# A narrow value granule and a narrow third q, k granule joined into one wide granule beside the scan

## The chip, the core and the metric

The kernel runs on one core of one Trainium2 chip. The metric is the device time of one execution in microseconds (us), taken several times; smaller is better. The engines are called PE (TensorE: matmuls and transposes), PEld (its weight loads), DVE (VectorE), ACT (ScalarE), POOL (GpSimd) and SP (SyncE, which here only issues DMAs).

## The reference

One decoder layer on 512 tokens of width 1024. After an RMS norm there is one input projection `h @ w_in`, whose columns go to a state-space branch, to dilated attention and to gates:

```python
h = rms_norm(x, norm_w[layer])
proj = h @ w_in[layer].astype(f32)
u_s, z_s, q, k, v, z_a, r_s, r_a = jnp.split(proj, offsets, axis=-1)
y_s = s5_branch(u_s, ...)                          # scan over the tokens, GELU, GLU with w_glu
y_s = (y_s * jax.nn.silu(z_s)) @ w_ssm_out[layer]
q = apply_partial_rope(rms_norm(q.reshape(head_shape), q_norm_w ...), positions)
k = apply_partial_rope(rms_norm(k.reshape(head_shape), k_norm_w ...), positions)
y_a = dilated_attention(q, k, v)                   # 3 groups of 8 heads, head size 64
y_a = (y_a * jax.nn.silu(z_a)) @ w_attn_out[layer]
m = jax.nn.sigmoid(r_s) * y_s + jax.nn.sigmoid(r_a) * y_a
x = x + m @ w_o[layer]
```

Everything is float32. The attention has three groups of heads (0 is local, 1 and 2 are dilated), and the heads are worked on in four pairs.

## The kernel before

**Products.** Each float32 factor is split into a high and a low part, and a product is three matmuls, `mm3` (L133 to L136): high by high, high by low, low by high. Three kinds of work unit do the projection.

- `cm_unit` (L255) gives 128 output columns for all 512 tokens: 8 steps in the contraction by 3 matmuls, each 512 wide, with a piece of the weights standing in the array. It fills one PSUM bank. The units are called by name: `u`, `za`, `zs`, `v0`, `rs`, `ra`.
- `wide_granule` (L958) gives 512 output columns as tokens by columns: four steps of weights (`kq`) by four blocks of 128 tokens (`r`) by 2 by 3 matmuls, each 512 wide, 96 in all. Four PSUM banks stay open through it.
- `tok_granule` (L670) does the same for only 256 output columns: two steps (`kh`) by four blocks by 4 by 3 matmuls, each 256 wide, again 96 in all, in two banks.

**Weights.** `plan` (L138 to L188) lists all pieces of weights, 512 KB each, in the order of use. `get_w` (L195) takes the next one and asks for two more in advance: a DMA on SP into `w_raw` (two buffers, L210), the high part on ACT (L250), the low part on DVE (L252), both into three buffers.

**Order of work.** PE follows the order of the code strictly (`follow`, L62). The other engines' orders are planned at build time by the framework, which simulates a timeline and fills each queue as work becomes ready there. In the first half the list `order` (L161) strings projection units together, and `events` (L935 to L946) hangs pieces of the state-space branch between them at numbered places: a `cm_unit` has four places, a `tok_granule` eight. The scan itself is a chain on DVE (`step`, L732) beside the units `zs`, `v0` and `v`; from place Y0 = 88 on, `chunk` (L906) computes the outputs of the scan and turns and gates them. The last units there are `rs0` to `rs7` and `ra0`, `ra1`, the merge gates, which ACT puts through tanh and SP stores to DRAM (`gd` for rs, `rad` for ra).

**PSUM.** Eight banks are dealt round (`deal`, L85): three to projections (`p`) and five to the rest (`g`) in the first half; four and four from L1192 on.

**The middle.** At L1193 to L1242 the norm weights of q and k are fetched: broadcast for the rotary tables `tC`, `tS` (built on POOL, L1238 to L1242), and as six rows in `wq` (L1220 to L1223), which `turn_wcol` (L1224) turns into columns by one PE transpose of a 6 by 128 tile, in the second unit of the next loop. That loop (L1246 to L1256) is the GLU: 8 units with `w_glu`, whose results `yT` need `zl` (the stored z, read back, L1248) multiplied on POOL (L1250, L1251). Eight units with `w_ssm_out` follow (L1258 to L1262).

**Attention.** `qk_first` (L1028) is a wide granule for q and k of groups 0 and 1 of a head pair, with copies out of PSUM, sums of squares, and the norm and rotation on DVE (`qk_norm`, L978). For pairs 1 to 3 `qk_second` (L1040) is a second wide granule with q, k of group 2 and v of groups 1 and 2. For pair 0 this work is in two narrow pieces: `v_granule` (L698), beside the scan, and `qk_third` (L1053), right behind `qk_first`. Behind `qk_third` comes the unit `ra2`, with the transposes of q and k of group 0 (`qk_turn`, L1003) at its last place, and then the wide granule of pair 1, with the transposes of group 1, scores and softmax of pair 0 at its places (`scoring_first`, L1302).

Of the kernel before, what the change touches and what calls it, by code (L numbers as in the profile page):

```python
# [11 lines left out]
F32 = mybir.dt.float32  # L12
# [8 lines left out]
P = 128  # L21
D = 1024
S = 512
KT = D // P
NB = S // P
# [9 lines left out]
NG = 3  # L35
U0, ZS0, Q0, K0, V0, ZA0, RS0, RA0 = 0, 1024, 2048, 3584, 5120, 6656, 7168, 8192
# [16 lines left out]
def tile_hybrid_block(ctx: ExitStack, tc: tile.TileContext, x, positions, norm_w, w_in, lam_re, lam_im,  # L53
# [3 lines left out]
    act, dve, pool, sp = nc.scalar, nc.vector, nc.gpsimd, nc.sync  # L57
# [25 lines left out]
    dram = ctx.enter_context(tc.tile_pool(name="dram", bufs=1, space=DRAM))  # L83
    psum = ctx.enter_context(tc.tile_pool(name="psum", bufs=1, space=PSUM))
    deal = {"p": [0, 1, 2], "g": [3, 4, 5, 6, 7]}  # L85
# [22 lines left out]
    def bank(name):  # L108
        return ps_tile("g", name)

    def pj_tile():
        return ps_tile("p", "pj")

    def t2k(name, dtype=F32):
        return tmp.tile([P, 512], dtype, name=name, tag="t2k")
# [17 lines left out]
    def mm3(o, lh, ll, rh, rl, first, last):  # L133
        pe.matmul(o, lh, rh, start=first, stop=False, skip_group_check=True)
        pe.matmul(o, lh, rl, start=False, stop=False, skip_group_check=True)
        pe.matmul(o, ll, rh, start=False, stop=last, skip_group_check=True)  # L136

    plan, loaded, look = [], [], 2  # L138
    n_ra = 2
    WARM = 38  # L140

    def call(at, i):
        for n, f in at:
            if n == i:
                f()

    def section(w, k0, k1, *cols):
        return [w[0][k0 * P:k1 * P, c:c + n] for c, n in cols]

    def cm_spec(w, c0, kts=KT):  # L150
        return (section(w, 0, kts, (c0, P)), kts, P)

    def tok_spec(w, *cols):
        return [(section(w, 4 * h, 4 * h + 4, *cols), 4, 256) for h in range(2)]

    def wide_spec(w, *cols):
        return [(section(w, 2 * h, 2 * h + 2, *cols), 2, 512) for h in range(4)]

    for c in range(KT):
        plan.append(cm_spec(w_in, U0 + c * P))  # L160
    order = [("za", c) for c in range(NP)] + [("zs", c) for c in range(KT)] + [("v0", 0), ("v", 0)]  # L161
    order += [("rs", c) for c in range(KT)] + [("ra", c) for c in range(n_ra)]
    for kind, c in order:
        if kind == "v":
            plan += tok_spec(w_in, (V0 + 512, P), (V0 + 1024, P))
        else:
            plan.append(cm_spec(w_in, {"za": ZA0, "zs": ZS0, "rs": RS0, "ra": RA0, "v0": V0}[kind] + c * P))
    for c in range(KT):
        plan.append(cm_spec(w_glu, c * P))
    for c in range(KT):  # L170
        plan.append(cm_spec(w_ssm_out, c * P))
    def head(base, g, hp):
        return (base + g * 512 + hp * P, P)

    for hp in range(NP):
        plan += wide_spec(w_in, head(Q0, 0, hp), head(K0, 0, hp), head(Q0, 1, hp), head(K0, 1, hp))
        if hp == 0:
            plan += tok_spec(w_in, head(Q0, 2, hp), head(K0, 2, hp))
            plan.append(cm_spec(w_in, RA0 + n_ra * P))
        else:  # L180
            plan += wide_spec(w_in, head(Q0, 2, hp), head(K0, 2, hp), head(V0, 1, hp), head(V0, 2, hp))
            plan.append(cm_spec(w_in, V0 + hp * P))
# [12 lines left out]
    def get_w():  # L195
        i = taken[0]
        taken[0] += 1
        prefetch(i + 1 + look)
        return loaded[i]
# [66 lines left out]
    ident = cst.tile([P, P], F32, name="ident")  # L266
# [12 lines left out]
    hT_hi = cst.tile([P, KT, S], F32R, name="hT_hi")  # L279
    hT_lo = cst.tile([P, KT, S], F32R, name="hT_lo")  # L280
# [360 lines left out]
    def ra_unit(c, at=()):  # L641
        ps = cm_unit(hT_hi, hT_lo, at=at)
        th = gate_tile() if c <= n_ra else t2k("th")
        act.activation(th, ps, AF.Tanh, scale=0.5)
        sp.dma_start(rad[c], th)
# [21 lines left out]
    maskB_f = maskB.rearrange("p a k -> p (a k)")  # L667


    def tok_granule(at=()):  # L670

        pss = [pj_tile() for _ in range(2)]
        for kh in range(2):
            hi, lo = get_w()
            for b in range(2):
                for rr in range(2):
                    call(at, 4 * kh + 2 * b + rr)
                    r = 2 * b + rr
                    o = pss[b][:, rr * 256:(rr + 1) * 256]
                    for k in range(4):  # L680
                        kk = 4 * kh + k
                        mm3(o, hT_hi[:, kk, r * P:(r + 1) * P], hT_lo[:, kk, r * P:(r + 1) * P],
                            hi[:, k], lo[:, k], kh == 0 and k == 0 and rr == 0, kh == 1 and k == 3)
        return pss

    def v0_unit(hp, V, at=()):
# [8 lines left out]
            act.copy(V[:, 0].rearrange("p b c -> p (b c)"), pt)  # L695
        return finish

    def v_granule(hp, V, at=()):  # L698
        pss = tok_granule(at)
        for b in range(2):  # L700
            act.copy(V[:, 1:3, 2 * b:2 * b + 2], pss[b].rearrange("p (r g c) -> p g r c", r=2, g=2))

    def new_v():
        return big.tile([P, NG, NB, P], F32, name="V", tag="s6a")
# [69 lines left out]
    V = new_v()  # L774
    fin = []

    def filler(kind, c, at):
        if kind == "v0":
            fin.append(v0_unit(0, V, at))
        elif kind == "v":  # L780
            v_granule(0, V, at)
        else:
            {"u": u_unit, "za": za_unit, "zs": zs_unit, "rs": rs_unit, "ra": ra_unit}[kind](c, at=at)

    Mb = [dd[:, o:o + 1024].rearrange("p (g k) -> p g k", g=8) for o in (0, 1024, 2048)]
    idp = ident.rearrange("p (m two q) -> p two m q", two=2, q=Q)
# [159 lines left out]
    events = [e for _, e in events]  # L946
    b0 = 0
    for kind, c in [("u", j) for j in range(3, 8)] + order:
        n = 8 if kind == "v" else 4
        filler(kind, c, [(b - b0, f) for b, f in events if b0 <= b < b0 + n])  # L950
        b0 += n
    for b, f in events:
# [1 line left out]
    gT_hi, gT_lo = gTs  # L954
    if "gT" in dbg:
        sp.dma_start(dbg["gT"], gT_hi.bitcast(F32).rearrange("p k s -> p (k s)"))

    def wide_granule(th, tl, at=(), halved=False):  # L958

        pss = [pj_tile() for _ in range(NB)] + ([bank("pj")] if halved else [])  # L960
        for kq in range(4):
            hi, lo = get_w()
            for r in range(NB):
                call(at, 4 * kq + r)
                parts = [(pss[r], slice(0, 512))]
                if halved and r == NB - 1:
                    parts = [(pss[r], slice(0, 256)), (pss[NB], slice(256, 512))]
                for ps, c in parts:
                    for k in range(2):
                        kk = 2 * kq + k  # L970
                        mm3(ps[:, c], th[:, kk, r * P:(r + 1) * P], tl[:, kk, r * P:(r + 1) * P], hi[:, k, c], lo[:, k, c],
                            kk == 0, kk == KT - 1)
        return pss

    def new_raw(i):
        return big.tile([P, NB, 256], F32, name="qraw", tag=("s7a", "s7b")[i])
# [43 lines left out]
    def squares(sq, src):  # L1020
        n = src.shape[1]
        s = t2k("qsq")
        act.activation(s[:, 0:n], src, AF.Square)
        sv = s[:, 0:n]
        sv = sv.rearrange("p (h d) -> p h d", d=HD) if len(sq.shape) == 2 else sv.rearrange("p (r h d) -> p r h d", r=2, d=HD)
        dve.tensor_reduce(sq, sv, AX.X, ALU.add)
# [25 lines left out]

    def qk_third():  # L1053

        pss = tok_granule()
        raw = ptb[:, 0:2].rearrange("p a (b c) -> p (a b) c", c=256)
        sq = sml.tile([P, NB, 8], F32, name="ssq")[:, :, 0:4]
        for b in range(2):
            act.copy(raw[:, 2 * b:2 * b + 2].rearrange("p r c -> p (r c)"), pss[b])
            squares(sq[:, 2 * b:2 * b + 2], pss[b])  # L1060
        qk_norm((2,), [raw], sq)
        return raw

# [129 lines left out]
    rt, qt = t2k("rope"), t2k("qkw")  # L1193
# [23 lines left out]
    sp.dma_start(qkw[:, 1].rearrange("p g d -> p (g d)"),  # L1217
                 k_norm_w[0].rearrange("g d -> (g d)").unsqueeze(0).to_broadcast([P, NG * HD]))
    dve.tensor_scalar(qkw[:, 0], qkw[:, 0], -0.125, None, op0=ALU.mult)
    wq = qt[0:2 * NG, 384:512]  # L1220
    for a, w in enumerate((q_norm_w, k_norm_w)):
        for h in range(2):
            sp.dma_start(wq[a * NG:a * NG + NG, h * HD:h * HD + HD], w[0])  # L1223
    def turn_wcol():  # L1224
        wps = bank("wcp")
        pe.transpose(wps[:, 0:2 * NG], wq, ident[:2 * NG, :2 * NG])
        for a in range(2):
            dve.tensor_scalar(wcol[:, :, a], wps[:, a * NG:a * NG + NG], (-0.125, 1.0)[a], None, op0=ALU.mult)
        pool.memset(wcol[0:16], 1.0)
        pool.memset(wcol[64:80], 1.0)  # L1230
# [15 lines left out]
    for c in range(KT):  # L1246
# [5 lines left out]
        ps = cm_unit(gT_hi, gT_lo, at=[(2, turn_wcol)] if c == 1 else ())  # L1252
        th = t2k("gth")
# [4 lines left out]
    for c in range(KT):  # L1258
        r = t2k("rl")
        sp.dma_start(r, gd[1, c])  # L1260
        ps = cm_unit(yT_hi, yT_lo)
# [17 lines left out]
    ptb = big.tile([P, 4, 512], F32, name="ptb", tag="s6b")  # L1279
# [8 lines left out]
    Vs = {0: V}  # L1288
    raws = qk_first()
    raw = qk_third()  # L1290

    def turn(hp, g, a):
        return lambda: qk_turn(g, (raws[0], raws[1], raw)[g], *QK, turned=(a,))

    ra_unit(n_ra, [(3, turn(0, 0, 0)), (3, turn(0, 0, 1))])

    def scoring(hp, n, fin):
# [15 lines left out]
    for hp in range(NP):  # L1313
        if hp < NP - 1:
            raws = qk_first(scoring(hp, 3, fin) if hp else scoring_first(4))
            n = 3
            at = turning(hp, n) + [(n + 5, lambda hp=hp: values(hp))]
# [3 lines left out]
        else:  # L1321
# [3 lines left out]
            at = scoring(hp, 3, fin) + turning(hp, 16)  # L1325
# [9 lines left out]
    for cc in range(KT // 2):  # L1335
        hi, lo = get_w()
        pss = [pj_tile() for _ in range(2)]
# [6 lines left out]
        for c2 in range(2):  # L1344
            c = 2 * cc + c2
            if c in rals:
                th = rals[c]
            else:
                th = t2k("ral")
# [43 lines left out]
```

## Time and profile before

| what | value |
|---|---|
| runs, median (lowest to highest of 3) | 675.36 us (675.04 to 675.65) |
| the profiled execution's own time | 675.1 us |
| its span in the profile | 673.1 us |
| PE busy | 665.6 us, 99% of the span |
| DVE busy | 463.8 us, 69% |
| ACT busy | 322.6 us, 48% |
| POOL busy | 116.1 us, 17% |

The span is the time in which the program's instructions run; the execution's own time has 2.0 us more around it. In the timeline a row is: start, duration, engine, source line, operation, written tile, read tiles, shape, count, and in brackets the idle time ahead of it with what ended it. Matmuls overlap, so what one costs is read from the distance between two starts, not from its duration. Line numbers are those of the kernel before.

### The profile page before, as it was taken

What the parts mean: (1) busy time and instruction counts of PE and PEld (TensorE: products, weight loads), DVE (VectorE), ACT (ScalarE), POOL (GpSimd) and SP (SyncE); (2) the same over time, 40 slices, a digit from 0 to 9 for tenths busy, and PEclk for the clock granted to TensorE, in tenths of its full rate; (3) what the DMA queues carried; (4) which work ended last, traced back from release to release, by engine and by line L of the source; (5) the groups of instructions that cost most, each with busy time, mean ns of one, the idle gap of its engine ahead of it and who ended that gap; (6) DMA issues with size and microseconds to landing.
All of it is one profiled execution on the core that took longest, in us unless ns stands there. A gap on an engine that the chain in (4) does not pass through costs nothing.

```text
span 673.1 us, 12602 instructions
## 1 busy us (share of the span) xinstructions
PE 665.6 (99%) x4785; PEld 563.4 (84%) x4785; DVE 463.8 (69%) x965; ACT 322.6 (48%) x676; POOL 116.1 (17%) x273
## 2 busy tenths in 40 slices
PE   8999999999999999999999999999999999999997
PEld 8988888889887888888889888888888888888886
DVE  7999989999787365843248776658566856666631
ACT  6645544323566562421444664557356645633310
POOL 1010000600365238600000030012001200210000
PEclk9999999999999999999999999999999999999999
DMA  9666424643665543573243423223232213247231
GB/s 310 130 163 164 115 85 134 169 145 106 156 148 145 132 138 93 188 237 103 68 125 86 119 64 96 62 64 91 67 94 63 85 42 95 94 151 272 94 125 63
DMA packets 137380, 82.13 MB, mean 122 GB/s; under 512 B 32736, under 2 KB 125928, under 8 KB 137192
## 3 DMA queue, kind: packets, MB, share of 16 engines
q1 hardware_dynamic: 134968, 78.31, 39.6%
q0 software_dynamic: 2048, 2.36, 2.2%
q8 instruction: 38, 0.62, 0.4%
q10 hardware_dynamic: 304, 0.66, 0.3%
q14 instruction: 22, 0.18, 0.1%
HBM read 68.46 MB, written 10.49 MB: 117 GB/s over the span
## 4 chain that ended last, share of the span: by engine, by line
PE 88%; DVE 4%; issue 2%; POOL 2%; ACT 2%; DMA 1%; SPq 0%; ACTq 0%; POOLq 0%; DVEq 0%
PE pj L69 73%; PE sps L69 3%; PE yps L69 2%; PE ot L69 2%; PE ptp L74 2%; PE qtp L74 2%; DVE w_lo L252 1%; PE xps L69 1%; ACT w_hi L250 1%; PE wps L74 1%; DVE gth L1255 1%; DMA x_all<-in_x_dram 1%; PE kps L69 1%; DMA qkw<-in_q_norm_w_dram 1%; PE yT L74 0%
## 5 line engine op out<-in xcount | busy, mean ns | idle before, releaser
L250 ACT ACTIVATE w_hi<-w_raw 128x1024 fp32r<-128x1024 f32 x94 | 99.4, 1058 | 153.6 <-PE pj L69 130.9
L252 DVE TENSOR_TENSOR w_lo<-w_raw,w_hi 128x1024 fp32r<-128x1024 f32 x94 | 118.1, 1258 | 60.2 <-ACT w_hi L250 59.6
L69 PE MATMUL pj<-hT_hi,w_hi 128*128 128x512 f32 (+1 forms) x344 | 131.4, 384 | 0.0
L69 PE MATMUL pj<-hT_lo,w_hi 128*128 128x512 f32 (+1 forms) x344 | 128.8, 376 | 0.4 <-DVE hT_lo L355 0.4
L69 PE MATMUL pj<-hT_hi,w_lo 128*128 128x512 f32 (+1 forms) x344 | 126.7, 375 | 0.0
L69 PE MATMUL pj<-w_hi,hT_hi 128*128 128x512 f32 (+1 forms) x288 | 108.7, 377 | 0.0
L69 PE MATMUL pj<-w_hi,hT_lo 128*128 128x512 f32 (+1 forms) x288 | 105.6, 367 | 0.0
L69 PE MATMUL pj<-w_lo,hT_hi 128*128 128x512 f32 (+1 forms) x288 | 105.5, 366 | 0.0
L69 PEld LDWEIGHTS pj<-hT_hi,w_hi 128*128 128x128 f32 x344 | 64.7, 188 | 12.6 <-issue 1.3
L69 PEld LDWEIGHTS pj<-hT_lo,w_hi 128*128 128x128 f32 x344 | 64.8, 188 | 11.1 <-DVE hT_lo L355 0.6
L69 PEld LDWEIGHTS pj<-hT_hi,w_lo 128*128 128x128 f32 x344 | 63.7, 188 | 11.8
L69 PEld LDWEIGHTS pj<-w_hi,hT_lo 128*128 128x128 f32 x288 | 54.3, 189 | 9.1
L69 PEld LDWEIGHTS pj<-w_hi,hT_hi 128*128 128x128 f32 x288 | 54.4, 189 | 8.5 <-issue 0.5
L69 PEld LDWEIGHTS pj<-w_lo,hT_hi 128*128 128x128 f32 x288 | 54.5, 189 | 7.5
L1117 POOL COPY sw<-st 32x4 f32<-32x4 f32 x64 | 11.9, 186 | 175.0 <-ACT Pt L1073 172.2
L1018 DVE SCALAR_TENSOR_TENSOR qkp<-qtp,wcol,qkp 128x512 fp32r<-128x512 f32 (+1 forms) x32 | 23.6, 748 | 25.3 <-ACT qkp L1017 25.2
L1073 ACT ACTIVATE Pt<-Pt,st 128x256 f32<-128x256 f32 (+1 forms) x64 | 30.9, 484 | 19.8 <-DVE st L1071 19.8
L837 POOL DMA_DIRECT2D dd<-kt x64 | 33.8, 537 | 2.4 <-POOL kt L833 2.1
L1017 ACT ACTIVATE qkp<-qtp,wcol 128x512 fp32r<-128x512 f32 (+1 forms) x32 | 21.2, 683 | 23.0 <-PE qtp L74 20.8
L69 PE MATMUL pj<-w_lo,mT_hi 128*128 128x512 f32 (+1 forms) x72 | 26.3, 366 | 0.0
L69 PE MATMUL pj<-w_hi,mT_hi 128*128 128x512 f32 (+1 forms) x72 | 26.3, 366 | 0.0
L69 PE MATMUL pj<-w_hi,mT_lo 128*128 128x512 f32 (+1 forms) x72 | 26.3, 365 | 0.0
(299 smaller groups left out, 1180.6 us busy)
## 6 DMA issues: line engine op xcount, KB each, us to landing
w_raw<-in_w_in_dram SPq DMA_DIRECT2D x36, 512.0 KB
w_raw<-in_w_in_dram SPq DMA_DIRECT2D x112, 128.0 KB
w_raw<-in_w_glu_dram SPq DMA_DIRECT2D x8, 512.0 KB
w_raw<-in_w_ssm_out_dram SPq DMA_DIRECT2D x8, 512.0 KB
w_raw<-in_w_o_dram SPq DMA_DIRECT2D x8, 512.0 KB
w_early<-in_w_in_dram SPq DMA_DIRECT2D x4, 512.0 KB
ud<-uT SPq DMA_DIRECT2D x8, 256.0 KB
uss<-ud SPq DMA_DIRECT2D x8, 256.0 KB
```

The lines of the kernel that those rows point to most:

```text
L69: last[0] = nc.tensor.matmul(*a, **k)
L74: last[0] = nc.tensor.transpose(*a, **k)
L250: last_act[0] = act.activation(hi, raw, AF.Copy).ins
L252: dve.tensor_tensor(lo, raw, hi.bitcast(F32), op=ALU.subtract)
L837: pool.dma_start(M[Q * t:Q * t + Q, :, 0:P - Q * t], kt[:, :, t:].rearrange("q g k p -> q g (k p)"))
L1017: act.activation(hi, ps[sl], AF.Copy, scale=w)
L1018: dve.scalar_tensor_tensor(lo, ps[sl], w, hi.bitcast(F32), op0=ALU.mult, op1=ALU.subtract)
L1073: act.activation(o, o, AF.Exp, bias=nm, scale=-1.0, accum_out=st[:, kind, 1, h, b:b + 1])
L1117: pool.tensor_copy(sw[32 * r:32 * r + 32, :, :, b], st[32 * b:32 * b + 32, 1, :, :, r])
L1255: dve.scalar_tensor_tensor(th, th, 1.0, z, op0=ALU.add, op1=ALU.mult)
```

## The change

- In the first half the narrow value granule is replaced by a wide one, `qv_granule`, at the same place of the list. Its 512 columns are q and k of group 2 and v of groups 1 and 2 of pair 0. For its duration banks are dealt four and four. It has 16 places in place of eight. Its q, k half is copied to SBUF and stored to a DRAM tile `qd`, two DMAs of 256 KB; its v half is copied to `V` as before, in four copies in place of two.
- `qk_third` loses its granule: it reads `qd` back into the tile where its copies went before, and takes the sums of squares from there.
- The gate units `ra0` and `ra1` leave the end of the list; they now stand between `qk_first` of pair 0 and `ra2`. `rs6` and `rs7` come last in the list, and all events keep their place numbers.
- `wq` becomes a tile of 128 rows, set to zero by a memset on POOL ahead of its four small DMAs, and the transpose takes the whole 128 by 128 tile.
- `wide_granule` moves up in the file unchanged; `tok_granule` and `tok_spec` go.

```diff
-    order += [("rs", c) for c in range(KT)] + [("ra", c) for c in range(n_ra)]
+    order += [("rs", c) for c in range(KT)]
     for kind, c in order:
         if kind == "v":
-            plan += tok_spec(w_in, (V0 + 512, P), (V0 + 1024, P))
+            plan += wide_spec(w_in, head(Q0, 2, 0), head(K0, 2, 0), head(V0, 1, 0), head(V0, 2, 0))
...
         if hp == 0:
-            plan += tok_spec(w_in, head(Q0, 2, hp), head(K0, 2, hp))
-            plan.append(cm_spec(w_in, RA0 + n_ra * P))
+            plan += [cm_spec(w_in, RA0 + c * P) for c in range(n_ra + 1)]
...
-    def v_granule(hp, V, at=()):
-        pss = tok_granule(at)
+    qd = dram.tile([2, P, 512], F32, name="qd")
+
+    def qv_granule(V, at=()):
+        few = dict(deal)
+        deal.update(p=[0, 1, 2, 3], g=[4, 5, 6, 7])
+        pss = wide_granule(hT_hi, hT_lo, at)
+        deal.update(few)
         for b in range(2):
-            act.copy(V[:, 1:3, 2 * b:2 * b + 2], pss[b].rearrange("p (r g c) -> p g r c", r=2, g=2))
+            qs = t2k("qs")
+            for i in range(2):
+                r = 2 * b + i
+                act.copy(qs[:, 256 * i:256 * i + 256], pss[r][:, 0:256])
+                act.copy(V[:, 1:3, r], pss[r][:, 256:512].rearrange("p (g c) -> p g c", g=2))
+            sp.dma_start(qd[b], qs)
...
-        n = 8 if kind == "v" else 4
+        n = 16 if kind == "v" else 4
...
     def qk_third():
-        pss = tok_granule()
         raw = ptb[:, 0:2].rearrange("p a (b c) -> p (a b) c", c=256)
+        for b in range(2):
+            sp.dma_start(ptb[:, b], qd[b])
         sq = sml.tile([P, NB, 8], F32, name="ssq")[:, :, 0:4]
         for b in range(2):
-            act.copy(raw[:, 2 * b:2 * b + 2].rearrange("p r c -> p (r c)"), pss[b])
-            squares(sq[:, 2 * b:2 * b + 2], pss[b])
+            squares(sq[:, 2 * b:2 * b + 2], ptb[:, b])
...
-    wq = qt[0:2 * NG, 384:512]
+    wqt = qt[:, 384:512]
+    pool.memset(wqt, 0.0)
+    wq = wqt[0:2 * NG]
...
-        pe.transpose(wps[:, 0:2 * NG], wq, ident[:2 * NG, :2 * NG])
+        pe.transpose(wps[:, 0:P], wqt, ident)
...
+    for c in range(n_ra):
+        ra_unit(c)
     ra_unit(n_ra, [(3, turn(0, 0, 0)), (3, turn(0, 0, 1))])
```

More of the change, by code (lines that the diff above doesn't have):

```diff
@@ L151, in cm_spec @@
         return (section(w, 0, kts, (c0, P)), kts, P)
-    def tok_spec(w, *cols):
-        return [(section(w, 4 * h, 4 * h + 4, *cols), 4, 256) for h in range(2)]
     def wide_spec(w, *cols):
@@ L160, in tile_hybrid_block, with head @@
         plan.append(cm_spec(w_in, U0 + c * P))
+    def head(base, g, hp):
+        return (base + g * 512 + hp * P, P)
     order = [("za", c) for c in range(NP)] + [("zs", c) for c in range(KT)] + [("v0", 0), ("v", 0)]
-    order += [("rs", c) for c in range(KT)] + [("ra", c) for c in range(n_ra)]
+    order += [("rs", c) for c in range(KT)]
     for kind, c in order:
         if kind == "v":
-            plan += tok_spec(w_in, (V0 + 512, P), (V0 + 1024, P))
+            plan += wide_spec(w_in, head(Q0, 2, 0), head(K0, 2, 0), head(V0, 1, 0), head(V0, 2, 0))
         else:
@@ L171, in tile_hybrid_block @@
         plan.append(cm_spec(w_ssm_out, c * P))
-    def head(base, g, hp):
-        return (base + g * 512 + hp * P, P)
     for hp in range(NP):
@@ L667, in tile_hybrid_block, with wide_granule @@
     maskB_f = maskB.rearrange("p a k -> p (a k)")
-    def tok_granule(at=()):
-        pss = [pj_tile() for _ in range(2)]
-        for kh in range(2):
+    def wide_granule(th, tl, at=(), halved=False):
+        pss = [pj_tile() for _ in range(NB)] + ([bank("pj")] if halved else [])
+        for kq in range(4):
             hi, lo = get_w()
[L675 to L683, printed above, removed]
+            for r in range(NB):
+                call(at, 4 * kq + r)
+                parts = [(pss[r], slice(0, 512))]
+                if halved and r == NB - 1:
+                    parts = [(pss[r], slice(0, 256)), (pss[NB], slice(256, 512))]
+                for ps, c in parts:
+                    for k in range(2):
+                        kk = 2 * kq + k
+                        mm3(ps[:, c], th[:, kk, r * P:(r + 1) * P], tl[:, kk, r * P:(r + 1) * P], hi[:, k, c], lo[:, k, c],
+                            kk == 0, kk == KT - 1)
         return pss
@@ L780, in filler @@
         elif kind == "v":
-            v_granule(0, V, at)
+            qv_granule(V, at)
         else:
-            {"u": u_unit, "za": za_unit, "zs": zs_unit, "rs": rs_unit, "ra": ra_unit}[kind](c, at=at)
+            {"u": u_unit, "za": za_unit, "zs": zs_unit, "rs": rs_unit}[kind](c, at=at)
     Mb = [dd[:, o:o + 1024].rearrange("p (g k) -> p g k", g=8) for o in (0, 1024, 2048)]
@@ L956, in tile_hybrid_block @@
         sp.dma_start(dbg["gT"], gT_hi.bitcast(F32).rearrange("p k s -> p (k s)"))
[L958 to L973, printed above, removed]
     def new_raw(i):
```

## The prediction

> **What bounds the kernel now.** First the page's head and its busy table.
>
> ```profile
> span 673.1 us, 12602 instructions
> PE 665.6 (99%) x4785; PEld 563.4 (84%) x4785; DVE 463.8 (69%) x965; ACT 322.6 (48%) x676; POOL 116.1 (17%) x273
> ```
>
> PE is idle for 7.5 us in all, so only PE's own work, or a wait on PE that grows, can move the end. Next the busy time by windows, for the narrow value granule, the wide `qk_first` of pair 0 and the narrow third granule. The window edges are starts of PE rows, so a window's length is what that granule costs PE.
>
> ```profile
> core 0: us, PE busy (x) PEld busy (x) DVE busy (x) ACT busy (x) POOL busy (x), PEclk, DMA share, GB/s
> 147.65:159.59 11.94, 11.94 (x101) 11.94 (x100) 11.35 (x13) 3.75 (x5) 0.00 (x0) 1.00 0.44 134
> 330.68:352.44 21.76, 21.76 (x97) 18.02 (x96) 6.87 (x7) 12.44 (x21) 0.00 (x0) 1.00 0.32 94
> 352.44:363.95 11.51, 11.51 (x97) 11.51 (x96) 10.15 (x24) 4.24 (x7) 0.00 (x0) 1.00 0.25 70
> ```
>
> All three are PE without a gap, at a full granted clock (1.00). 96 matmuls 512 wide take 21.76 us, 0.2267 each; 96 that are 256 wide take 11.51 us, 0.1199 each, a little over half. The first window holds four transposes more (`vtp`, the finish of `v0`), whence 11.94. Last the chain of work that ended last, in order of time.
>
> ```profile
> 151.12 19.54 PE pj L69 x120
> ...
> 236.90 1.07 ACT w_hi L250
> 237.99 1.24 DVE w_lo L252
> 239.67 0.57 SPq L1205
> 240.29 4.21 DMA qkw<-in_q_norm_w_dram
> ...
> 291.27 0.70 DVE yT_lo L123
> 292.01 76.21 PE pj L69 x380
> ```
>
> Through both places where narrow granules stand (147 to 160 and 352 to 364) the chain is PE itself. Between 236.90 and 292.01 it is not: it leaves PE at the end of the last unit but one, and runs through a weight load and the position and norm-weight loads on SP (by the code, the rotary tables on POOL and the GLU's POOL work hang on these) to the low part of `yT`, and back to PE at 292.01.
>
> **The change part by part. The granules.** Removed are 192 narrow matmuls, 2 x 11.51 = 23.02 us of PE; added are 96 wide ones, 21.76 us. That is 1.26 us less PE work: half of the matmuls, each of which carries a fixed part. (The two widths give it: 0.2267 - 2 x 0.1199 = -0.013, so 13 ns a matmul, and 96 fewer are 1.26 us.) `ra0` and `ra1` cost the same wherever they stand. By place: up to the end of the list PE loses the narrow 11.51 and two units of 24 x 0.2267 = 5.44, and gains 21.76, so it gets there 0.63 us earlier; behind `qk_first` it loses 11.51 and gains 10.88, again 0.63.
>
> The Trainium skill prices this otherwise: "TensorE: Matmul & The Clock Gate", section "Back-to-back issue gap", gives a warm gap of N / 2.4 + 2.5 ns, which as an estimate makes 0.109 and 0.216 us of the two widths and 0.24 us of this part. The trace's 0.1199 and 0.2267 do not agree, and they decide; what is left of it is rival 4.
>
> **The whole turn of the norm weights.** The timeline of PE at that transpose, and at the four full transposes in the value granule:
>
> ```profile
> 250.79 0.39 PE L69 MATMUL pj<-gT_hi,w_lo 128*128 128x512 f32 x1
> 251.11 0.22 PE L74 MATMUL wcp<-ident,qkw 6*128 6x6 f32 x1
> 251.26 0.50 PE L69 MATMUL pj<-gT_hi,w_hi 128*128 128x512 f32 x1
> 251.60 0.39 PE L69 MATMUL pj<-gT_lo,w_hi 128*128 128x512 f32 x1
> ```
>
> ```profile
> 150.52 0.60 PE L74 MATMUL vtp<-ident,vt 128*128 128x128 f32 x4
> 150.88 0.36 PE L69 MATMUL pj<-w_hi,hT_hi 128*128 128x256 f32 x1
> 151.07 0.28 PE L69 MATMUL pj<-w_lo,hT_hi 128*128 128x256 f32 x1
> ```
>
> From 250.79 to 251.60 there are 0.81 us where two matmul steps take 0.45: the six-row transpose costs 0.36. From 150.52 to 151.07 there are 0.55 us, of which one narrow step is 0.12: four full transposes cost 0.43, 0.11 each. So PE saves 0.25 us. But this lies in the stretch where the chain is not PE, and the weight loads of PE show its end:
>
> ```profile
> 292.01 0.19 PEld L69 LDWEIGHTS pj<-yT_lo,w_hi 128*128 128x128 f32 x1 [0.52 <-DVE yT_lo L123]
> ```
>
> PE waits there for the last low part of `yT`, and nothing in that chain reads the turned weights on the way. If PE arrives 0.25 earlier, the wait becomes 0.77. I take nothing for this edit; its bounds are 0 and -0.25. The memset on POOL stands ahead of the four small loads on SP, behind which wait the first `zl` load and the next weights:
>
> ```profile
> 239.96 1.29 POOL L1250 TENSOR_TENSOR gsum<-gT_hi,gT_lo 128x512 f32<-128x512 f32 x1 [15.12 <-issue]
> ```
>
> POOL is idle for 15 us ahead of this, so the memset runs as soon as its buffer is free; even behind this row it would hold SP up by no more than its 1.29 us, which the 4.21 us of the `qkw` load above, the one the tables wait for, hides.
>
> **The wide granule beside the scan.** Three things could stall PE. First, four banks in place of two. The deal's count puts the first tile into the bank of `zs7`, whose last reader is a DVE row, in a stretch where DVE is 95% busy (11.35 of 11.94). Second, the scan must be done by `chunk(0)`, and third, the coefficients for the kernels `kps` behind it.
>
> ```profile
> 145.13 0.68 DVE L621 SCALAR_TENSOR_TENSOR z<-th,pj 128x512 f32<-128x512 f32 x1
> ...
> 164.50 0.69 DVE L742 TENSOR_TENSOR Xs<-Xs,scn 128x512 f32<-128x512 f32 x1
> ...
> 169.83 0.76 DVE L424 TENSOR_TENSOR ab<-ab 128x576 f32<-128x576 f32 x1
> ```
>
> ```profile
> 171.91 1.16 PE L69 MATMUL yps<-ab,Xs 64*64 64x64 f32 x64
> 173.00 0.66 PE L69 MATMUL kps<-ab,dd 64*16 64x128 f32 x32
> ```
>
> The bank is free at 145.81 and needed at 147.65: 1.84 us to spare, and nothing ahead of it changes. The scan ends at 165.19 and is needed at 171.91, the coefficients end at 170.59 and are needed at 173.00: 6.7 and 2.4 us to spare, less the 0.63 that PE comes earlier. DVE has as many low parts to make per us as before. All three cost nothing; the last, with 1.8 us left, would be next to show.
>
> The copies out of PSUM become eight of half the width:
>
> ```profile
> L1049 ACT COPY V<-pj 128x256 f32<-128x256 f32 x12 | 4.6, 383 | 0.0
> ```
>
> 8 x 0.383 = 3.06 us of ACT, which was busy for 3.75 of 11.94. The first bank is dealt again to `rs0`, but its last matmul lies 3 x 1.36 = 4.08 us ahead of that, time for its two copies. The two stores of `qd` stand on SP like the gate stores, ahead of weight pieces that are needed two units (10.9 us) later. Nothing on the path: 0.
>
> **Behind `qk_first`.** Its norm must be done at the transposes of group 0:
>
> ```profile
> 363.30 0.41 DVE L1001 TENSOR_TENSOR qraw<-rt,rt 128x256 f32<-128x256 f32 x1
> ```
>
> ```profile
> 368.07 1.03 PE L74 MATMUL qtp<-ident,qraw 128*128 128x128 f32 x8
> ```
>
> It has 4.4 us to spare; PE comes 0.63 us earlier, 3.7 are left, while the third's squares, sums and norm may now start sooner and stand between. Two sums of squares already do. The loads of `qd` wait for stores of 190 us ago. Cost 0; what is left of DVE's load moves off the start of pair 1, where PE does not wait for it.
>
> **Sum.** -1.26 us from the granules and 0 from all else. The profiled execution took 675.1 us, 673.1 in the span and 2.0 around it, 0.3 below the median of 675.36 and within its runs. From the median: 675.36 - 1.26 = 674.1 us, -0.19%. A measurement of this kernel can tell some 0.2%, 1.35 us, from no change; the forecast lies just short of that line, 674.01.
>
> **The rivals.**
> 1. *The turn counts too.* If the stretch up to 292 is a little shorter in the new order, PE's 0.25 us and part of the 0.52 wait come on top: 675.36 - 1.26 - 0.25 = 673.85, and at best 673.3, with all of the 0.52. For it: the wait is small. Against: the chain is tied to the same PE event as before.
> 2. *Slower: the z loads wait for the gate stores.* `rs7` now stores into `gd` at the end of the list, just before the first `zl` load reads the same DRAM tile; before, `ra1` stored to another tile there. If the load were held until that store has landed, the chain would lengthen:
>
> ```profile
> 243.45 0.35 SPq L1248 DMA_DIRECT2D zl<-gd  x1
> 245.31 0.35 SPq L645 DMA_DIRECT2D rad<-th  x1
> ```
>
> ```profile
> 246.33 2.23 POOL L1251 TENSOR_TENSOR zl<-zl,gsum 128x512 f32<-128x512 f32 x1 [5.09 <-DMA zl<-gd]
> 249.61 0.25 POOL L1240 TENSOR_TENSOR tS<-rope,qkw 128x32 f32<-128x32 f32 x1 [1.05 <-ACT rope L509]
> ```
>
> A load takes 2.9 us from issue to use; I take the same for a store. All 0.63 earlier: store at 244.7, landed at 247.6, load used at 250.5, multiply done at 252.7. The tables stand behind it on POOL (second row), at 249.0 in the new order; they would start 3.7 us late, and PE's wait at 292 would grow by that: 674.1 + 3.7 = 677.8. The kernel is slower than before once they start over 1.3 us late. Against it, on the same queue at the read-back of `rad`:
>
> ```profile
> 369.42 0.47 SPq L1324 DMA_DIRECT2D th<-rad  x1
> 371.86 0.34 SPq L645 DMA_DIRECT2D rad<-th  x1
> ```
>
> There a load of one slice goes ahead of the store of another, so slices do not wait for each other.
> 3. *One stage gives its share back.* If DVE is late by 2.4 us or so beside the scan, or by over 3.7 behind `qk_first`, one of the 0.63 goes: 674.1 + 0.63 = 674.7.
> 4. *The wide matmuls are no cheaper there.* If beside the scan, with DVE 95% busy where the wide window has 32%, a wide matmul took as long as two narrow ones, 96 x 0.2398 = 23.02 us, the granules would give nothing: 675.4. Against it: the two narrow windows have DVE at 95% and 88%, and both run at 0.1199 (11.94 less the 0.43 of the transposes is 11.51). By the page named above it would be 675.36 - 0.24 = 675.1.
> 5. *No gain.* The queues are planned anew by the build's simulation; a wait of 1 to 2 us anywhere eats the gain: 675 to 676.
>
> **How the numbers follow.** Forecast 0.45, at 674.1, with a range of its own from 673.7 to 674.5 for the spread of the runs (0.3 us to either side of the median), and 0.21 of the 0.45 beyond the line of 674.01. Rival 1 0.25 (0.24 beyond the line), rival 2 0.07, rival 3 0.12, rival 4 0.04, rival 5 0.07, of which 0.04 is slower by over 0.2%. Faster by over 0.2%: 0.21 + 0.24 = 0.45. Slower: 0.07 + 0.04 = 0.11. Within: the rest, 0.44. The range of 673.2 to 675.7 reaches from the best of rival 1 to the middle of rival 5, and leaves out rival 2 and half of rival 5.
>
> **What would show it.** Right: no 256-wide rows at the value granule, whose window is 21.8 + 0.4 = 22.2 us without a PE gap; three `ra` units behind `qk_first`; `chunk(0)` some 0.6 us earlier, `qtp` of pair 0 some 1.3 earlier; the wait for `yT_lo` near 0.8; a whole transpose at 0.11. Wrong: a PE wait inside the wide granule or before `kps`, a wait at the first `qtp`, tables on POOL starting later than 249.0, or an end that moves by less than the two windows do.

## The result and the profile after

The changed kernel takes 672.58 us (median of 20 runs, 671.73 to 677.93) against 675.24 (20 runs, 674.30 to 678.72) for the kernel before beside it: 2.66 us less by the medians, which is a ratio of 0.9961. The ratio on record, which goes by more than the medians, is 0.9968 with an interval of 0.9953 to 0.9982, so a gain of 2.2 us, between 1.2 and 3.2. The forecast of 674.1 was too small a gain, and the result lies below its range. (The forecast's ratio, 0.9981, is just inside this interval; experiment 1, with 0.9943 to 0.9974, and the profiles show that the rest is real.) The profiled execution took 671.95 us, its span is 670.1 after 673.1. The page's head, and the window of the new granule with its four transposes:

```profile
span 670.1 us, 12439 instructions
PE 663.3 (99%) x4689; PEld 557.8 (83%) x4689; DVE 463.3 (69%) x965; ACT 322.7 (48%) x680; POOL 116.1 (17%) x274
```

```profile
core 0: us, PE busy (x) PEld busy (x) DVE busy (x) ACT busy (x) POOL busy (x), PEclk, DMA share, GB/s
147.71:169.96 22.25, 22.25 (x101) 18.22 (x99) 20.89 (x25) 7.22 (x12) 0.00 (x0) 1.00 0.36 106
```

PE has no gap in the wide granule, and 22.25 us is the 22.2 of the prediction, with DVE busy for 20.89 of them. PE's busy time is down by 2.3 us and its idle time by 0.7 (7.5 to 6.8), though its wait for `x` at the start is 0.5 longer in this execution.

To see where 3.0 us of span went, the chain is compared by stages: the starts of the same pieces, before and after, and what the changed kernel is ahead by.

| piece of the chain | before | after | ahead |
|---|---|---|---|
| outputs `yps` of `chunk(0)` | 171.04 | 170.50 | 0.54 |
| `yps` of `chunk(4)` | 206.12 | 205.58 | 0.54 |
| `yps` of `chunk(5)` | 214.82 | 212.92 | 1.90 |
| the chain leaves PE (`w_hi` on ACT) | 236.90 | 235.01 | 1.89 |
| back on PE behind `yT_lo` | 292.01 | 289.83 | 2.18 |
| first `qtp` of pair 0 | 368.23 | 365.42 | 2.81 |
| last long stretch of PE | 603.59 | 600.80 | 2.79 |

The two lots of the granules are there: 0.54 in the first half (0.60 from the starts of the two granules, 147.65 and 147.71; 0.63 was worked out) and 0.63 between 292 and 368. The surprise is 1.36 us between two chunks, in code that the change does not touch. There, the chain of before, and then that of the changed kernel (start, length, what, number of instructions):

```profile
206.12 2.02 PE yps L69 x96
208.14 0.34 PE kps L69 x10
208.49 0.96 issue
209.45 0.62 PE kps L69 x22
210.07 4.32 PE pj L69 x18
```

```profile
205.58 2.02 PE yps L69 x96
207.60 0.59 PE kps L69 x32
208.19 4.30 PE pj L69 x18
```

In the kernel before, PE stops after 10 of the 32 small matmuls `kps` and waits for nothing that the profile knows ("issue"). From the start of `kps` to the next `pj` it takes 1.93 us (208.14 to 210.07), in the changed kernel 0.59: the stop costs 1.34 us. The profile of before had shown it: the full chain has the row of 0.96 us, and the list of PE's waits has this line as the second of its four (us in total, times, longest), which is missing in the list of the changed kernel:

```profile
PE kps L69 <- issue: 1.0, 1, 1.0
```

So 1.26 + 1.34 = 2.60 us, near the 2.66 of the medians and inside the interval of 1.2 to 3.2, which is too wide to tell more. The GLU stretch gave 0.29 more in the two profiled executions; experiment 1 shows that this part changes from one execution to another.

The theory to test: the stop is a late fetch of PE's own instructions. In the DMA records a queue marked "instruction" brings PE's program in packets of 16 KB, one for each 256 instructions, and a matmul is two instructions (load and multiply). In the trace the stop at `kps` always lies at PE's instruction 4033, counted from 0 in order of start; the stops of experiments 10 and 12 below lie at 4289, one block of 256 later. The DMA by queue of the kernel before, from PE's entry into the block ahead (instruction 3777, at 203.55) on, in two windows, 203.55 to 206.95 and 206.95 to 209.45:

```profile
q0 software_dynamic: 95, 0.17, 43.4%
q1 hardware_dynamic: 266, 0.33, 29.0%
```

```profile
q1 hardware_dynamic: 1140, 0.51, 71.4%
q0 software_dynamic: 139, 0.11, 13.7%
q8 instruction: 1, 0.02, 2.2%
```

In the first 3.4 us no instruction packet is moved; the packet starts at 207.00, lasts 0.88 us, and 1.57 us after its end PE goes on, at 209.45. In the chunks, whose 128 tiny matmuls are 256 instructions, a block is used up in about 5 us (203.55 to 208.49); between them 24 large matmuls, 48 instructions, take 5.44. The change moves where the blocks end: the wide granule has 16 places where the narrow one had eight, so the chunks stand two units, 96 instructions, earlier in PE's program. The rivals: the matmuls `kps` themselves, the queues as planned anew, the gate units' new place, or data on the DMA engines.

### The profile page after: what moved, and what is told of

It is laid out like the page before. It is cut to its first block, busy times and chain, and to the rows that moved or that the text cites. A ratio compares the mean times of both kernels' runs of the same rounds, so it can differ in the third digit from the quotient of the medians.

```text
span 670.1 us, 12439 instructions
## 1 busy us (share of the span) xinstructions
PE 663.3 (99%) x4689; PEld 557.8 (83%) x4689; DVE 463.3 (69%) x965; ACT 322.7 (48%) x680; POOL 116.1 (17%) x274
## 4 chain that ended last, share of the span: by engine, by line
PE 88%; DVE 4%; issue 2%; DMA 2%; ACT 2%; POOL 1%; SPq 0%; ACTq 0%; DVEq 0%; POOLq 0%
PE pj L69 73%; PE sps L69 3%; PE yps L69 2%; PE ot L69 2%; PE ptp L74 2%; PE qtp L74 2%; DVE w_lo L248 1%; PE xps L69 1%; ACT w_hi L246 1%; PE wps L74 1%; DVE gth L1247 1%; DMA x_all<-in_x_dram 1%; PE kps L69 1%; DMA qkw<-in_q_norm_w_dram 1%; PE yT L74 0%
## 5 line engine op out<-in xcount | busy, mean ns | idle before, releaser
L69 PE MATMUL pj<-w_hi,hT_hi 128*128 128x512 f32 x256 | 103.1, 403 | 0.0
L69 PE MATMUL pj<-w_hi,hT_lo 128*128 128x512 f32 x256 | 100.0, 390 | 0.0
L69 PE MATMUL pj<-w_lo,hT_hi 128*128 128x512 f32 x256 | 99.9, 390 | 0.0
L69 PEld LDWEIGHTS pj<-w_hi,hT_lo 128*128 128x128 f32 x256 | 48.0, 188 | 10.3
L69 PEld LDWEIGHTS pj<-w_hi,hT_hi 128*128 128x128 f32 x256 | 48.1, 188 | 9.6 <-issue 0.5
L69 PEld LDWEIGHTS pj<-w_lo,hT_hi 128*128 128x128 f32 x256 | 48.2, 188 | 8.7
```

The costliest lines, as they stand in the source:

```text
L69: last[0] = nc.tensor.matmul(*a, **k)
```

## The experiments

**1 and 2. One part at a time.** The changed kernel with the six-row transpose put back, and the kernel before with the whole one.

```diff
...
-        pe.transpose(wps[:, 0:P], wqt, ident)
+        pe.transpose(wps[:, 0:2 * NG], wq, ident[:2 * NG, :2 * NG])
```

> The kernel after, with the six-row turn of the norm weights put back (no memset, a 6 by 128 transpose). It separates the two edits. If the turn's 0.25 us of PE time is swallowed by the wait for the last low part of yT, as the prediction took it, the time is that of the kernel after, 672.6, within 0.1; the wait falls from 0.5 to some 0.25. If the turn counts, the time is 672.8 to 672.9. In both cases the 0.96 us gap of PE in the middle of the kps matmuls at 208.5 stays away, because the number of PE instructions ahead of it is that of the kernel after.

> The kernel before, with only the whole turn of the norm weights. The gap of 0.96 us at kps (209.45) stays, since nothing ahead of it changes. If the yT chain swallows the turn: 675.2, the same as before, with a yT_lo wait of 0.77 in place of 0.52. If the turn counts: 675.0. Nothing here can explain more than 0.25 us.

Without the whole turn: 672.82 us (7 runs), ratio to before 0.9958 (0.9943 to 0.9974). With it alone: 674.81 (12 runs), 0.9999 (0.9985 to 1.0013). The turn is worth nothing that can be measured, and the whole gain is the granule's and the gate units'. In the first of them PE has gaps of 0.36 and 0.22 us at the end of the GLU (290.66 and 291.39), with another releaser (`yT_hi`, 0.8 us) than the changed kernel's `yT_lo`: this end moves by tenths from one execution to another. The stop at `kps` is gone in the first and there in the second (0.69 us, again at instruction 4033).

**3 and 4. Other instruction counts ahead of the chunks.** More of the transposes that warm PE up at the start: 48 more in the changed kernel, which puts back the 96 instructions that it has lost ahead of the chunks; 80 more (118 in place of 38) in the kernel before.

```diff
-    WARM = 38
+    WARM = 86
```

> The kernel after, with 48 more warm-up transposes at the start (86 in place of 38): as many PE instructions more as the list has fewer ahead of chunk 0 in the new order (two units of 24). Theory, late instruction fetch: the gap inside kps depends on where the blocks of PE's instructions begin against the dense small matmuls of the chunks; with the old count restored the gap of about 1 us comes back in the same chunk. Then the time is 672.6 + 48 x 0.11 - 1.3 (PE's idle time ahead of hps) + 1.4 = 678.0. Rival, the gap came of what the other queues and DMAs did at that moment in the old order: these are as in the kernel after, so no gap, and 676.6.

> The kernel before, with 80 more warm-up transposes (118 in place of 38): 160 PE instructions, which in blocks of 256 puts the chunks where they stand in the kernel after (96 fewer). Late instruction fetch: the gap inside kps goes, and the time is 675.2 + 80 x 0.11 - 0.8 - 1.4 = 681.8. Rival, the old order of transfers makes the gap: it stays at kps of the same chunk, and the time is 683.2.

The changed kernel takes 678.73 us (8 runs; 1.0056, 1.0036 to 1.0076), and the stop is back, at instruction 4033 as before:

```profile
213.21 0.41 PE L69 MATMUL kps<-ab,dd 64*16 64x128 f32 x10
214.86 0.62 PE L69 MATMUL kps<-ab,dd 64*16 64x128 f32 x22 [1.24 <-issue]
```

The kernel before takes 682.23 us (4 runs; 1.0102, 1.0081 to 1.0124), and its stop is gone, with nothing of the chunks changed:

```profile
215.99 0.66 PE L69 MATMUL kps<-ab,dd 64*16 64x128 f32 x32
216.57 0.50 PE L69 MATMUL pj<-hT_hi,w_hi 128*128 128x512 f32 x1
```

So it is the position in PE's program, in both directions. `kps` as such, the wide granule and the new queues are out as causes: experiment 4 has the narrow granules and the old queues, experiment 3 the new ones. The times lie nearer to this theory's 678.0 and 681.8 than to 676.6 and 683.2.

**5 and 6. The data of the weight load.** The load of 512 KB that SP issues at 204.45 us, just after PE has entered block 3777, is doubled by a copy into a tile that nobody reads, and then cut to an eighth. The second of these leaves out seven eighths of the weights of the gate unit `ra1`.

```diff
...
+        if i == 32:
+            spare = dram.tile([KT * P, P], F32, name="spare")
+            with tc.issue_after(d.ins):
+                sp.dma_start(spare, srcs[0])
```

```diff
+        if i == 32:
+            sp.dma_start(raw[:, 0:1], srcs[0][0:P].rearrange("(k p) c -> p k c", p=P))
+            raw = raw[:, 0:1].broadcast_to([P, kts, cols])
...
```

> The kernel before, with a second copy of the weight piece that is loaded at 204.45 us (512 KB, from DRAM to DRAM, into a spare tile that nothing reads) issued on SP just behind that load; PE's instructions and all other queues are as before. Theory (PE's 0.96 us gap at its instruction 4033 is a late fetch of instructions, held up by the data on the DMA engines): before, the packet of the fetch starts 3.45 us after PE has entered the block ahead; with twice the data from 204.5 us on it starts 1 to 2 us later, the gap grows to 2 to 3 us, and the kernel takes 676.2 to 677.2 us. If fetch packets go ahead of data that is already queued, the gap stays and so does the time. Rival (the gap is something of the matmuls kps themselves, or of the position in the program alone): gap 1.0, 675.2.

> The kernel before, where that same load at 204.45 us brings an eighth of the piece (64 KB in place of 512) and the split reads that eighth eight times; it leaves out seven eighths of the weights of one gate unit. PE's instructions and the order of all queues are as before. Theory (late fetch behind data): the packet of the fetch starts 1 to 2.5 us after PE has entered the block ahead, as most do, the gap of 0.96 us is gone or under 0.2, and the kernel takes 674.2 to 674.4. Rival (kps itself or the position alone): gap 1.0, 675.2.

Neither moved the fetch as the theory had it. With twice the data 676.40 us (10 runs; 1.0015, 1.0000 to 1.0029), which is inside the 676.2 to 677.2 expected, but not by a longer stop; with an eighth 675.43 (10 runs; 1.0001, 0.9988 to 1.0014). The packet starts 3.40 and 3.67 us after PE's entry (3.45 before), and the stop is 0.69 and 0.96 us. So the fetch is not late because of this load, and that half of the theory fell. It does not clear data on the DMA engines in general: from PE's entry to the start of the packet, the hardware queue q1 moved 0.34 MB before, 0.30 in experiment 5 and 0.32 in experiment 6, so the two edits hardly changed the data ahead of the packet.

**7 and 8. The gate units' place, and the place of the chunks.** The changed kernel with `ra0`, `ra1` back at the end of the list; and that kernel with the chunks eight places later, so that as many PE instructions stand ahead of each as before.

```diff
-    order += [("rs", c) for c in range(KT)]
+    order += [("rs", c) for c in range(KT)] + [("ra", c) for c in range(n_ra)]
...
-    for c in range(n_ra):
-        ra_unit(c)
...
```

```diff
-    W0, K0B, V0B, Y0 = 16, 49, 74, 88
+    W0, K0B, V0B, Y0 = 16, 49, 74, 96
```

> The changed kernel with its two gate units put back to the end of the list beside the scan, so of the change the wide granule and the whole turn remain. The wide granule takes 16 places of the list where the narrow one took 8, so the chunks still stand two units earlier than before and PE's instructions up to the last chunk are those of the changed kernel. Theory (late fetch, set by where the blocks of instructions end): no gap at kps, 672.6 us like the changed kernel, and 672.1 to 672.6 if the wait for the low part of yT goes, since PE has two units more ahead of it. Rival (the gate units' place is what took the 1.4 us away): the gap is back and the kernel takes 673.6 to 674.0.

> The kernel of the run above (wide granule, gate units in the list), with the chunks eight places of the list later, so that they stand between the same units as before and as many PE instructions stand ahead of each as before. Theory (late fetch): the gap is back at instruction 4033, 0.7 to 1.4 us, and the kernel takes 673.3 to 674.0 us, which is the kernel before less the 1.26 us of the granules. Rival (the wide granule or the new queues took the gap away): no gap, 672.6.

On the stop both expectations hold: none in the first, and in the second

```profile
218.50 0.41 PE L69 MATMUL kps<-ab,dd 64*16 64x128 f32 x9
219.88 0.62 PE L69 MATMUL kps<-ab,dd 64*16 64x128 f32 x23 [0.97 <-issue]
```

On the times both miss by far: 680.52 us (4 runs; 1.0074, 1.0051 to 1.0096) and 682.20 (4 runs; 1.0101, 1.0073 to 1.0128), both slower than the kernel before. Most of the cause stands in one row of PE's timeline (experiment 7):

```profile
371.64 1.94 PE L74 MATMUL qtp<-ident,qraw 128*128 128x128 f32 x8 [6.46 <-DVE qa L129]
```

With nothing but three quarters of one unit between `qk_first` and the transposes of group 0, PE waits 6.46 us for the norm and rotation on DVE. Behind this wait the granted clock is 0.50 instead of 1.00 until 375.89 (third figure from the end):

```profile
371.64:375.89 4.25, 4.25 (x14) 3.61 (x15) 3.89 (x15) 1.52 (x3) 0.00 (x0) 0.50 0.00 0
```

From these transposes to the next ones (375.92) PE takes 4.28 us, in the changed kernel 2.26 (365.26 to 367.52): another 2.0 us. Wait and clock make some 8.5 us in this execution; by the medians experiment 7 takes 7.9 us more than the changed kernel. In experiment 8 the wait is as long, and the granted clock stays at 0.50 until 379.02. Before, the narrow third granule (11.5 us) stood there; the change fills the place with the two gate units (10.9 us). That is what "gate units in their place" is worth: without it, the wide granule makes the kernel 5.4 us slower than before.

**9 and 10. POOL's transfers later.** Something else stands at the same place in the six kernels with the stop above (before, experiments 2, 3, 5, 6 and 8): POOL issues eight transfers of the kernel block `kt` into `dd`, and PE enters block 3777 0.3 to 0.6 us after their start.

```profile
202.96 4.21 POOL L837 DMA_DIRECT2D dd<-kt  x8 [0.30 <-POOL kt L833]
```

Here POOL first multiplies that block (j = 5) by 1.0, twice, in the kernel before and in the changed one.

```diff
+        if j == 5:
+            for _ in range(2):
+                pool.tensor_scalar(kt, kt, 1.0, None, op0=ALU.mult)
         M = Mb[j % 3]
```

> The kernel before, in which POOL multiplies the fifth kernel block kt by 1.0 twice before it issues that block's eight transfers into dd, so that this issuing (202.96 to 207.17 us before, 4.21 us) starts some 2 to 4 us later; PE's instructions are as before. Theory (the late fetch stands behind POOL's issuing: in all six kernels with the gap POOL starts those eight transfers 0.3 to 0.6 us before PE enters block 3777, and the packet of the fetch starts 3.9 to 4.3 us after POOL does): the packet now starts 0.5 to 2.5 us after PE has entered the block, the gap at instruction 4033 is gone, and the kernel takes 674.1 to 674.4 us. Rivals (the position of the block alone, or something of kps): packet at +3.4 us, gap 0.7 to 1.0, 675.2.

> The changed kernel with the same two multiplications on POOL. There POOL issues the eight transfers from 202.42 to 206.61 us and PE enters block 3777 only at 206.12, whose fetch starts 1.92 us later. Theory (a fetch stands behind POOL's issuing): POOL now starts at 204.5 to 206.5 and ends at 208.7 to 210.7, the packet starts 2.5 to 4.5 us after PE has entered the block in place of 1.92, and as this block lasts 6.7 us PE still has no gap, or one under 0.5: 672.6 to 673.0. Rival (POOL's issuing is beside the point): packet at about +2, 672.6.

The two multiplications take 6.01 us, more than meant, so POOL starts at 209.01 and 208.60, and the outputs of `chunk(5)` wait for the late block: 676.96 us (12 runs; 1.0014, 1.0001 to 1.0027) and 679.05 (4 runs; 1.0052, 1.0034 to 1.0070). PE's wait for it is 1.8 and 1.7 us in the two traces, and in both the granted clock is 0.50 for 3.4 us soon after (from 216.64 and 220.31). So the times, which were expected at 674.1 to 674.4 and 672.6 to 673.0, say nothing of the fetch; the traces do. In the kernel before, the packet starts 2.08 us after PE's entry, and `kps` runs through:

```profile
208.02 0.66 PE L69 MATMUL kps<-ab,dd 64*16 64x128 f32 x32
```

In the changed kernel the packet of block 3777 starts at +2.06 us, ahead of POOL's begin at 208.60; the number given for it (2.5 to 4.5) missed. But at the next block a stop of 1.99 us appears that this kernel did not have (instruction 4289): POOL issues from 213.59 to 217.77, PE enters block 4033 at 215.01, the packet starts at 217.58.

**11 and 12. The same with one multiplication**, 3.16 us.

> The kernel before with one multiplication of the fifth kt by 1.0 on POOL in place of the two of the run before: by that run's 6.01 us for two it takes 3.0 us, so POOL issues its eight transfers from 206.0 to 210.2 us and is free before its next block at 211.9; nothing else is moved. Theory (PE's fetch waits for POOL's issuing): the packet starts about 2 us after PE has entered block 3777 in place of 3.45, the gap of 0.96 us is gone or under 0.2, no new gap comes at 213 us, and the kernel takes 674.2 us, ratio 0.9986. Rival (the position alone): gap and 675.2 as before.

> The changed kernel with the same one multiplication. POOL issues from 205.4 to 209.6 us, PE enters block 3777 at 206.1 as in the changed kernel. Theory (a fetch that is asked for while POOL is issuing waits for the end of it): the packet starts at 209.4 to 209.8, 3.3 to 3.7 us after PE has entered the block in place of 1.92; the block lasts 6.7 us, so PE has no gap all the same, and the time stays at 672.6 to 672.9 us. Rival (POOL's issuing is beside the point): packet at about +2, 672.6.

The kernel before gains: 674.40 us (11 runs; 0.9982, 0.9969 to 0.9995), with the packet at +2.08 us and no stop at 4033. It is a gain by a useless instruction, if a small one: the interval ends just short of 1. The profiled execution has a wait for the late block at `chunk(5)` in its place, so its span (673.5) does not show the gain:

```profile
215.03 1.15 PE L69 MATMUL yps<-dd,uss 128*64 128x64 f32 x32 [1.37 <-DMA dd<-kt]
```

The changed kernel takes 675.69 us (12 runs; 1.0011, 0.9991 to 1.0031): the packet for which the number was given starts at +2.48 us, not at 3.3 to 3.7, though PE enters its block (206.19) while POOL issues (205.76 to 209.99). That speaks against the theory as it was put. Of the time, some 2.2 us (215.72 to 218.13, less one step of 0.227) are lost at the next packet, where POOL issues from 211.61 to 215.78 and the packet starts at 215.60:

```profile
215.72 0.49 PE L69 MATMUL pj<-hT_hi,w_hi 128*128 128x512 f32 x1
218.13 0.50 PE L69 MATMUL pj<-hT_lo,w_hi 128*128 128x512 f32 x1 [1.92 <-issue]
```

In five of these 12 runs the mean granted clock is 0.994 to 0.997, and they take 676.47 to 679.82 us; the profiled one has 1.000.

The eight stops side by side, from the traces (us; the last column is PE's idle time at the next block):

| kernel | POOL issues | PE enters the block | packet starts | PE stands |
|---|---|---|---|---|
| before | 202.96 to 207.17 | 203.55 | 207.00 | 0.96 |
| experiment 2 | 202.87 to 207.06 | 203.45 | 206.79 | 0.69 |
| experiment 3 | 208.18 to 212.37 | 208.46 | 212.48 | 1.24 |
| experiment 5 | 203.05 to 207.24 | 203.62 | 207.02 | 0.69 |
| experiment 6 | 203.28 to 207.47 | 203.80 | 207.47 | 0.96 |
| experiment 8 | 213.38 to 217.57 | 213.75 | 217.34 | 0.97 |
| experiment 10 | 213.59 to 217.77 | 215.01 | 217.58 | 1.99 |
| experiment 12 | 211.61 to 215.78 | 212.97 | 215.60 | 1.92 |

In all eight the packet starts between 0.3 us ahead of the end of POOL's issuing and 0.1 behind it. But this is no rule for all packets. Some start in the middle of the issuing: in the kernel before one at 189.96, with POOL issuing from 186.28 to 190.80; in the changed kernel one at 179.19, in 176.29 to 180.50. And some are as late without it: in experiment 1 PE enters a block at 215.66, POOL starts to issue at 218.68, and the packet starts at 219.52, 3.86 us after PE's entry; there is no stop, since that block lasts 9.3 us. So two things are shown: the packet comes late, at a place set by the position in the program (experiments 3, 4 and 8), and in the kernel before it comes in time when POOL's transfers come later (9 and 11). Still open is why it is late: whether POOL's issuing, the first data of these transfers or something else holds the fetch, and what lets one through. In the changed kernel PE enters block 4033 at 212.86 while POOL issues from 211.53 to 215.70, as in experiment 12, and yet the packet starts at 212.16, ahead of PE. In experiment 12 the packet of block 3777 starts 1.3 us ahead of POOL's end. A fetch asked for before POOL begins, and a PE that is held up by a late block of `dd` and asks later, might explain the two; that was not tried.

## Why the prediction was wrong

- **"PE is idle for 7.5 us in all, so only PE's own work, or a wait on PE that grows, can move the end."** This is the step that failed, with "0 from all else" in the sum. A wait on PE that shrinks moves the end too. Of the 7.5 us a part lies neither at the start nor at the end: 0.96 us inside `kps`, 1.34 by the starts. It depended on how many instructions stand ahead of the chunks, and the change took 96 of them away. The prediction searched the places that the change touches for waits and never asked what the idle time consisted of, though the line was in the list of PE's waits. Why the fetch is late there, and so whether the change could have been known to take the stop away, stays open.
- **The granules, -1.26 us.** Right: 0.54 and 0.63 in the stages, and no PE gap in the window of 22.25. Beside 1.34 it is half of the result. By the formula of the Trainium skill, "TensorE: Matmul & The Clock Gate", section "Back-to-back issue gap", both granules together would give 0.24 us, as an estimate; the section gives it for a single matmul by itself, and the 0.63 measured for the third granule alone does not agree with it.
- **The whole turn, 0 with bounds of 0 and -0.25.** Right in size: experiment 2 has 0.9999. The transpose itself costs 0.12 us in the changed kernel (0.11 was said): 0.57 from 248.90 to 249.47, less two steps of 0.227.

```profile
248.90 0.39 PE L69 MATMUL pj<-gT_hi,w_lo 128*128 128x512 f32 x1
249.13 0.27 PE L74 MATMUL wcp<-ident,qkw 128*128 128x128 f32 x1
249.16 0.48 PE L69 MATMUL pj<-gT_hi,w_hi 128*128 128x512 f32 x1
249.47 0.40 PE L69 MATMUL pj<-gT_lo,w_hi 128*128 128x512 f32 x1
```

  The wait for `yT_lo` was to be near 0.8 and is 0.49:

```profile
289.82 0.19 PEld L69 LDWEIGHTS pj<-yT_lo,w_hi 128*128 128x128 f32 x1 [0.49 <-DVE yT_lo L123]
```

  The chain from the last unit to it became 0.29 us shorter (55.11 to 54.82; the `qkw` load in it took 3.84 us after 4.21), which is rival 1 in this one execution. The runs of experiments 1 and 2 can't tell 0.25 us.
- **The wide granule beside the scan, 0.** Right: its window of 22.25 us has no gap, and rivals 3 and 4 are out.
- **Behind `qk_first`, 0, with 3.7 us left.** Right: there is no wait at the first `qtp`; 2.8 us were left (the rotation of group 0 ends on DVE at 362.43, the transposes start at 365.26). But the prediction took "`ra0` and `ra1` cost the same wherever they stand" from PE's work alone. Where they stand is a cover for a wait of 6.46 us, and for the 2.0 us at half the granted clock behind it (experiment 7).
- **Rival 2, the z loads,** did not come: the tables on POOL start at 247.36, ahead of the 249.0 of the prediction, and PE is back at 289.83, earlier by more than where it left.
- **Rival 5** had a wait of 1 to 2 us appear anywhere. Such a wait was there already, and went.

## What to carry to other kernels

On an engine that is busy for 99%, take the remaining idle time apart before saying what can move the end: each gap with its place and its releaser, the short ones too. A gap put down to "issue" in the middle of a run of small instructions may be a late fetch; look for the packet in the instruction queue, and at what POOL issues at that time. Such a gap can come and go with an edit that changes the number of instructions ahead of it, so as much of an edit's gain or loss may have nothing to do with what it was meant to do, and padding (experiments 3 and 4) tells the two apart. And a wait that an edit brings up on PE can cost more than its length: see the granted clock behind it (experiment 7).

## What the runs showed of the hardware

- PE's instructions come in packets of 16 KB for 256 instructions, which last 0.9 to 1.6 us in the stretch of the chunks. A block of tiny matmuls is used up in 2.9 to 5 us, and PE goes on 1.3 to 1.7 us after the late packet's end. The Trainium skill, "Runtime: NRT & Kernel Launch", section "Instruction fetch mechanics", describes blocks of 256 instructions that the sequencer fetches ahead, at a cost that is mostly hidden. The blocks agree with the trace; the cost was 0.7 to 2.0 us in the eight stops above.
- In the eight stops the late packet starts within 0.3 us of the end of POOL's issuing of eight transfers (4.2 us). Other packets start in the middle of such issuing, or as late without it, so what holds a fetch is not shown. Twice or an eighth of the data of one load on SP's queue moved the start of the packet by -0.05 and +0.22 us.
- Behind a wait of PE of 6.46 us the granted clock was 0.50 for the next 4.25 us (experiment 7), and it was 0.50 for 3.4 us soon after waits of 1.8 us (experiment 9), and of 1.7 and 2.0 us (experiment 10). In the traces of experiments 11 and 12, with waits of 1.4 and 1.9 us, it stayed at 1.00, so the length of the wait alone does not decide it; what does is not shown.
- Two multiplications on POOL of a tile of 16 partitions by 1024 take 6.01 us, one 3.16.
